# Silu, the convolution's first step and the cast of the gated product issued later, and the first pair's second tile read sooner

## The chip, the cores and the metric

The kernel runs on one core of a Trainium2 chip. The metric is the device time of one execution in microseconds (us). Engines are named as the profile names them: PE does the matmuls (PEld loads their weights), DVE the elementwise work, ACT the activations and plain copies, POOL small copies and sums, SP issues most DMAs. A tile in PSUM is where PE accumulates and where DVE and ACT read results; all other tiles here are in SBUF.

## What is computed

One step of one decoder layer for 512 prompt tokens and 64 sample tokens (8 sequences of 8), 576 columns in all. The change touches only the gated feed-forward part:

```python
h = _rmsnorm(x, norm2_w)
ua, ub = jnp.split(h @ w_up, [D_FF], axis=-1)          # D_MODEL 1024, D_FF 2816
buf = jnp.concatenate([conv_s0.astype(ua.dtype), ua], axis=1)
conv = conv_b
for j in range(CONV_W):                                # CONV_W = 3
    conv = conv + buf[:, j:j + T] * conv_w[j]
x = x + (jax.nn.silu(conv) * ub) @ w_down
```

Before it stand the input projection, retention, attention and the output projection; behind it the final norm.

## The kernel before

**Tiling.** Activations lie transposed: 128 channels on the partitions, 576 token columns. Every f32 matmul is done as three: weight and activation are split into a rounded part and a remainder (`whi`, `wlo`; `hhi`, `hlo` for the normed input; `bhi`, `blo` for the gated product), and PE does hi·hi, hi·lo and lo·hi, each on two halves of 288 columns. A pair of such matmuls is the unit of the traces below. ACT makes `whi` (L289), DVE makes `wlo` (L296); SP loads the raw weights (L250).

**The feed-forward** has 22 channel tiles `f`, in three groups of 8, 8 and 6. For each `f` PE makes two products with the up weights: the first tile (`pa`, the convolution's branch) and the second tile (`pb`, the gate). Tiles 0, 1 and the other odd ones go through `dense` (L341) into PSUM tiles `d`, of which there are two; their elementwise work is `up_post`. Tiles 2, 4, ... 20 (ten of them, called slabs here) go through `up_seven` (L1274), which trades an eighth matmul block for sums, into PSUM tiles `m`; their elementwise work is `post_seven`, and ACT copies parts of `m` out in between (L1280, L1282, L1286). When a group is through, `dense` multiplies its gated products by the down weights, one product (index `n`) after the other.

**The elementwise chain of one f**: `ue` = first tile times the token's norm factor `rstd_b` (L1337, L1338); the convolution's first step on ACT (L1341, in `post_seven` L1301); two more steps on DVE (L1345, L1346; L1310, L1311); Silu on ACT (L1348; L1313); `g` = second tile times `rstd_b` (L1353; L1314); the gated product (L1320, L1321); its cast `bhi` on ACT (L1323) and remainder `blo` on DVE (L1325). The norm factor itself comes from `norm2`: sums over channels, an inverse root, and a broadcast through PE (L415) that DVE copies out (L416, L417).

**What sets the order.** Instructions are not written down in running order. Each chain is a generator, and `Merge` runs them against a planned clock: `yield cost, delay` adds PE cost in ns to that clock and lets this chain go on only after `delay` ns more. Each engine then runs its own instructions strictly in the order in which they were emitted, and waits on semaphores where it must. A delay in a `yield` thus moves an instruction behind others on its engine; it makes nobody wait by itself. PSUM and SBUF slots are given out by the same order: a new `d` tile gets the slot whose last reader was emitted first.

```python
    def add(self, gen, left=None, delay=0.0):
        ...
            self.clock += c[0]
            e["at"] = self.clock + c[1]
```

Of the kernel before, what the change touches and what calls it, by code (L numbers as in the profile page):

```python
# [22 lines left out]
T = NP + NS  # L23
# [123 lines left out]
def decoder_step(ctx, tc, a):  # L147
    nc = tc.nc
    pe, dve, act, pool, sp = nc.tensor, nc.vector, nc.scalar, nc.gpsimd, nc.sync
# [24 lines left out]
    def f32(ap):  # L174
        return ap.bitcast(F32)
# [182 lines left out]
    def tok(ps):  # L358
        return ps[:, C0:C0 + T]
# [27 lines left out]
    rstd_b = cst.tile([P, T], F32, name="rstd_b")  # L387
# [18 lines left out]
    def rstd_cols(dst, ss, n):  # L406
        dve.tensor_scalar(ss, ss, 1.0 / n, EPS, op0=OP.mult, op1=OP.add)
        rsqrt(dst, ss, stat[:, 35:40])

    def row_broadcast(dst, cols):  # L410
        p1, p2 = mtile(), mtile()
        for j in range(5):
            r, s = rows_of(j)
            ps = p1[:, s] if j < 4 else p2[:, :NS]
            pe.transpose(ps, cols[:r, j:j + 1].to_broadcast([r, P]), ident[:r, :r])  # L415
        dve.tensor_copy(dst[:, :NP], p1)  # L416
        dve.tensor_copy(dst[:, NP:], p2[:, :NS])  # L417
# [195 lines left out]
    def keep_rows():  # L613
        if copies:
            act.dma_start(*copies.pop(0))
# [515 lines left out]
    def tmp(name):  # L1131
        return fp.tile([P, UE], F32, name=name, tag="tmp", bufs=6)
# [21 lines left out]
    def token_sums(dst, x):  # L1154
        dve.memset(dst, 1.0)
        ps = mtile()
        for j in range(5):
            r, s = rows_of(j)
            pe.matmul(ps[:r, j:j + 1], x[:, s], ones[:, 0:1], start=True, stop=True)
        dve.tensor_copy(dst[:, 0:4], ps[:, 0:4])  # L1160
        dve.tensor_copy(dst[:NS, 4:5], ps[:NS, 4:5])
# [14 lines left out]
    def norm2():  # L1176
        token_sums(ss2, acc)
        rstd_cols(stat[:, 20:25], ss2, D)
        yield 2200.0, 3700.0
        row_broadcast(rstd_b, stat[:, 20:25])  # L1180
        norm2_made.append(1)
        yield 550.0, 100.0
# [15 lines left out]
    def out_post(m, ps):  # L1198
# [15 lines left out]
        if last:  # L1214
            yield 0.0, 5000.0
            yield from norm2()
# [21 lines left out]
    def seqs(t, off, n):  # L1238
        return t[:, NP + 2:UE].rearrange("p (b t) -> p b t", b=B)[:, :, off:off + n]

    def by_seq(x):
        return x.rearrange("p (b t) -> p b t", b=B)

    def up(f, n, ghi, glo, made):
        if f in SEVEN:
            yield from up_seven(f, n, ghi, glo, made)
            return
        pa = dtile()
        yield from dense(pa, ("up", f), hhis, hlos, 0, KD, True, True, made=h_made)
        pb = dtile()  # L1250
        done = []
        mg.add(up_post(f, n, pa, pb, done, ghi, glo, made), None, 4000.0 if f == 0 else 0.0)
        yield from dense(pb, ("up", NF + f), hhis, hlos, 0, KD, True, True)
        done.append(1)

    def up_seven(f, n, ghi, glo, made):
# [7 lines left out]
        for q, (dst, c) in enumerate(order):  # L1264
            w_begin(j + q)
            if split[j + q][1] is None:
                w_mid(j + q)
            hi, lo = split.pop(j + q)
            xh, xl = TH[c]
            for k in range(4):  # L1270
                while c[0] == "T" and (c, k) not in t_made:
                    yield None
                for wt, b in ((hi, xh), (hi, xl), (lo, xh)):
                    pe.matmul(dst, wt[:, k], b[:, k], start=q in (0, 1, 2, 5) and k == 0 and wt is hi and b is xh,  # L1274
                              stop=k == 3 and wt is lo, skip_group_check=True)
                if k == 0:
                    w_mid(j + q)
                yield 394.0, 0.0
            if q == 0:
                act.copy(ts[0], pa)  # L1280
            elif q == 1:
                act.copy(ts[1], pc)  # L1282
            elif q == 2:
                dve.tensor_tensor(y[:, :H2], pb, ts[0], op=OP.add)
            elif q == 3:
                act.copy(ts[2], pa)  # L1286
            elif q == 4:
                dve.tensor_tensor(y[:, H2:T], pc, ts[2], op=OP.add)
                mg.add(post_seven(f, n, pa, ts[1], y, z, stage, ghi, glo, made))
            elif q == 5:  # L1290
                act.copy(z[:, :H2], pd)
        stage.append(1)

    def post_seven(f, n, pa, t, y, z, stage, ghi, glo, made):
        u, L = ues[f % 2], UE - 2
        pool.tensor_copy(seqs(u, 0, 2), by_seq(csT[:, f]))
        dve.tensor_mul(u[:, 2:NP + 2], y[:, :NP], rstd_b[:, :NP])
        dve.tensor_mul(seqs(u, 2, TS), by_seq(y[:, NP:T]), by_seq(rstd_b[:, NP:]))
        yield 0.0, 1100.0
        c = tmp("cv")  # L1300
        act.activation(c[:, :L], u[:, 0:L], AF.Identity, scale=convw[:, 0, f:f + 1], bias=convb[:, f:f + 1])  # L1301
        pool.tensor_copy(cout[:, 0:2, f], u[:, NP:NP + 2])
        pool.tensor_copy(by_seq(cout[:, 2:, f]), seqs(u, TS, 2))
        while not stage:
            yield None
        yield 0.0, 300.0
        dve.tensor_tensor(z[:, :H2], pa, z[:, :H2], op=OP.add)
        dve.tensor_tensor(z[:, H2:T], pa, t, op=OP.add)
        yield 0.0, 900.0
        dve.scalar_tensor_tensor(c[:, :L], u[:, 1:L + 1], convw[:, 1, f:f + 1], c[:, :L], op0=OP.mult, op1=OP.add)  # L1310
        dve.scalar_tensor_tensor(c[:, :L], u[:, 2:L + 2], convw[:, 2, f:f + 1], c[:, :L], op0=OP.mult, op1=OP.add)  # L1311
        yield 0.0, 1700.0
        act.activation(c[:, :L], c[:, :L], AF.Silu)  # L1313
        dve.tensor_mul(z[:, :T], z[:, :T], rstd_b)  # L1314
        yield 0.0, 900.0
        yield from gated(f, n, z, c, ghi, glo, made)

    def gated(f, n, g, c, ghi, glo, made):

        dve.tensor_tensor(g[:, :NP], g[:, :NP], c[:, :NP], op=OP.mult)  # L1320
        dve.tensor_tensor(by_seq(g[:, NP:T]), by_seq(g[:, NP:T]), seqs(c, 0, TS), op=OP.mult)  # L1321
        yield 0.0, 1000.0
        act.copy(ghi[n], g[:, :T])  # L1323
        yield 0.0, 1500.0
        dve.tensor_sub(glo[n], g[:, :T], f32(ghi[n]))  # L1325
        made[n] = 1
        up_made.append(f)
        if f % 2 == 0:
            keep_rows()

    def up_post(f, n, pa, pb, done, ghi, glo, made):
        u = ues[f % 2]
        ya, L = tok(pa), UE - 2
        while not norm2_made or not cs_made:
            yield None
        pool.tensor_copy(seqs(u, 0, 2), by_seq(csT[:, f]))
        dve.tensor_mul(u[:, 2:NP + 2], ya[:, :NP], rstd_b[:, :NP])  # L1337
        dve.tensor_mul(seqs(u, 2, TS), by_seq(ya[:, NP:]), by_seq(rstd_b[:, NP:]))  # L1338
        yield 0.0, 1800.0
        c = tmp("cv")  # L1340
        act.activation(c[:, :L], u[:, 0:L], AF.Identity, scale=convw[:, 0, f:f + 1], bias=convb[:, f:f + 1])  # L1341
        pool.tensor_copy(cout[:, 0:2, f], u[:, NP:NP + 2])
        pool.tensor_copy(by_seq(cout[:, 2:, f]), seqs(u, TS, 2))
        yield 0.0, 1800.0
        dve.scalar_tensor_tensor(c[:, :L], u[:, 1:L + 1], convw[:, 1, f:f + 1], c[:, :L], op0=OP.mult, op1=OP.add)  # L1345
        dve.scalar_tensor_tensor(c[:, :L], u[:, 2:L + 2], convw[:, 2, f:f + 1], c[:, :L], op0=OP.mult, op1=OP.add)  # L1346
        yield 0.0, 1300.0
        act.activation(c[:, :L], c[:, :L], AF.Silu)  # L1348
        while not done:
            yield None  # L1350
        yield 0.0, 1400.0
        g = tmp("g")
        dve.tensor_mul(g[:, :T], tok(pb), rstd_b)  # L1353
        yield 0.0, 1000.0
        yield from gated(f, n, g, c, ghi, glo, made)

    def conv_state_out():
# [175 lines left out]
```

## Time and profile before

| | us |
|---|---|
| median of 3 runs (824.2 to 825.31) | 824.35 |
| the profiled execution's own time | 825.07 |
| its span in the trace | 823.3 |
| PE busy, 6439 matmuls | 796.0 (97%) |
| DVE busy | 518.2 (63%) |
| ACT busy | 345.0 (42%) |
| down products of the three groups begin at | 493.11, 641.11, 764.84 |

The profiled execution's time is its span and 1.77 us around it. PE is busy nearly all the time, so a change can only gain where PE stands still or runs slowly, and can only lose by making it stand still. Of the views of the trace, the one that lists what PE waited for says where it stood still; the timeline of one engine gives the starts of its instructions, and the distance between two starts, against the same distance in an undisturbed stretch, is what a wait has cost, with the refilling of PE behind it. "Granted clock" in the view by stretches is the share of full speed that PE was given.

### The profile page before, as it was taken

How to read it: one execution, taken by the hardware profiler on the slowest of the kernel's cores; microseconds unless marked ns; L12 is line 12 of the kernel's file. 1: busy time of each engine (PE TensorE's matmuls, PEld its weight loads, DVE VectorE, ACT ScalarE, POOL GpSimd, SP SyncE). 2: the span in 40 equal slices, each digit the busy share in tenths (PEclk: the TensorE clock that was granted, in tenths of full speed). 3: DMA queues.
4: the chain of work that ended last, by engine and by line, in shares of the span. 5: the costliest groups of instructions: out<-in, count | busy, mean ns of one | idle time of the engine just before them, and what ended most of it. 6: DMA issues, size and time to landing. Idle time of an engine off the chain costs nothing.

```text
span 823.3 us, 16179 instructions
## 1 busy us (share of the span) xinstructions
PE 796.0 (97%) x6439; PEld 757.5 (92%) x6439; DVE 518.2 (63%) x1098; ACT 345.0 (42%) x691; POOL 99.0 (12%) x199
## 2 busy tenths in 40 slices
PE   7999999999999999999899999999999999999994
PEld 6999999887888888999799999999999999999994
DVE  5664555665646566787767875347878534778663
ACT  5423232454535567456334452124444312444522
POOL 1311202011110213022001100000110000110021
PEclk9999999999999999999989999999999999999997
DMA  9355653778887863427245554215545621544603
GB/s 268 110 171 140 191 178 96 187 208 220 224 246 207 224 172 103 122 87 251 77 153 180 180 179 152 79 53 179 180 135 174 205 77 52 180 136 147 214 1 115
DMA packets 179673, 128.68 MB, mean 156 GB/s; under 512 B 14849, under 2 KB 176273, under 8 KB 179086
## 3 DMA queue, kind: packets, MB, share of 16 engines
q1 hardware_dynamic: 178445, 93.75, 40.3%
q10 hardware_dynamic: 928, 33.63, 11.3%
q8 instruction: 51, 0.84, 0.4%
q0 software_dynamic: 224, 0.28, 0.1%
q14 instruction: 25, 0.20, 0.1%
HBM read 121.52 MB, written 39.66 MB: 196 GB/s over the span
## 4 chain that ended last, share of the span: by engine, by line
PE 83%; DVE 8%; ACT 3%; issue 3%; DMA 1%; POOL 0%; ACTq 0%; SPq 0%; DVEq 0%; POOLq 0%
PE d L341 52%; PE m L1274 11%; PE m L980 3%; PE d L546 2%; PE m L1025 2%; DVE wlo L296 1%; PE m L907 1%; PE d L990 1%; PE m L894 1%; PE m L593 1%; ACT whi L289 1%; PE px L505 1%; DVE blo L1325 1%; PE px L341 1%; PE m L763 1%
## 5 line engine op out<-in xcount | busy, mean ns | idle before, releaser
L341 PE MATMUL d<-bhi,whi 128*128 128x288 f32 x786 | 176.8, 306 | 2.9 <-ACT bhi L1323 1.7
L341 PE MATMUL d<-blo,whi 128*128 128x288 f32 x786 | 168.1, 295 | 0.8 <-DVE blo L1325 0.8
L341 PE MATMUL d<-bhi,wlo 128*128 128x288 f32 x786 | 168.1, 295 | 0.0
L341 PEld LDWEIGHTS d<-bhi,whi 128*128 128x128 f32 x786 | 124.6, 189 | 8.7 <-issue 3.1
L341 PEld LDWEIGHTS d<-blo,whi 128*128 128x128 f32 x786 | 126.0, 188 | 1.5 <-DVE blo L1325 1.5
L341 PEld LDWEIGHTS d<-bhi,wlo 128*128 128x128 f32 x786 | 126.2, 188 | 0.0
L296 DVE TENSOR_TENSOR wlo<-wraw,whi 128x512 fp32r<-128x512 f32 (+1 forms) x145 | 99.7, 705 | 39.5 <-ACT whi L289 39.3
L289 ACT ACTIVATE whi<-wraw 128x512 fp32r<-128x512 f32 (+1 forms) x145 | 87.3, 619 | 81.2 <-PE d L341 71.8
L341 PE MATMUL d<-hhi,whi 128*128 128x288 f32 x312 | 67.9, 299 | 4.4 <-DVE ue L1338 4.4
L341 PE MATMUL d<-hhi,wlo 128*128 128x288 f32 x312 | 67.7, 298 | 0.0
L341 PE MATMUL d<-hlo,whi 128*128 128x288 f32 x312 | 67.4, 298 | 0.0
L341 PEld LDWEIGHTS d<-hhi,whi 128*128 128x128 f32 x312 | 51.0, 192 | 4.9 <-issue 4.8
L341 PEld LDWEIGHTS d<-hlo,whi 128*128 128x128 f32 x312 | 50.8, 191 | 0.0
L341 PEld LDWEIGHTS d<-hhi,wlo 128*128 128x128 f32 x312 | 50.8, 191 | 0.0
L1274 PE MATMUL m<-T,whi 128*128 128x288 f32 x240 | 48.6, 295 | 0.0
L1389 DVE TENSOR_TENSOR xT<-d,xT 128x576 f32<-128x576 f32 x23 | 17.4, 757 | 40.7 <-PE d L341 40.7
L296 DVE TENSOR_TENSOR wlo<-wrawb,whi 128x512 fp32r<-128x512 f32 (+1 forms) x32 | 22.6, 713 | 28.7 <-ACT whi L289 28.7
L1274 PEld LDWEIGHTS m<-T,whi 128*128 128x128 f32 x240 | 38.4, 188 | 0.2 <-ACT ct L1280 0.2
L1274 PE MATMUL m<-T,wlo 128*128 128x288 f32 x120 | 35.5, 296 | 0.0
L1323 ACT CAST bhi<-g 128x576 fp32r<-128x576 f32 x22 | 14.8, 674 | 49.1 <-DVE g L1321 49.0
L888 POOL TENSOR_SCALAR s<-s,sc 128x128 f32<-128x128 f32 (+3 forms) x32 | 18.3, 579 | 140.4 <-DVE sc L886 125.8
L981 ACT COPY kt<-m 128x384 f32<-128x384 f32 x32 | 15.3, 478 | 39.3 <-PE m L980 37.2
(333 smaller groups left out, 1574.7 us busy)
## 6 DMA issues: line engine op xcount, KB each, us to landing
wraw<-in_w_up_dram SPq DMA_DIRECT2D x33, 512.0 KB, 3.7
wraw<-in_w_in_dram SPq DMA_DIRECT2D x26, 512.0 KB, 6.4
kc<-in_cache_win_k_dram SPq DMA_DIRECT2D x32, 256.0 KB, 3.5
vc<-in_cache_win_v_dram SPq DMA_DIRECT2D x32, 256.0 KB, 3.5
wraw<-in_w_down_dram SPq DMA_DIRECT2D x12, 512.0 KB, 3.5
wrawb<-in_w_up_dram SPq DMA_DIRECT2D x11, 512.0 KB
kc<-in_cache_win_k_dram SPq DMA_DIRECT2D x64, 64.0 KB, 3.3
vc<-in_cache_win_v_dram SPq DMA_DIRECT2D x64, 64.0 KB, 3.1
```

What stands on the lines that cost most here:

```text
L289: act.activation(split[j][0][:, :n], src, AF.Copy)
L296: dve.tensor_sub(split[j][1][:, :n], src, f32(split[j][0][:, :n]))
L341: pe.matmul(ps[:, C0 + s * H2:C0 + (s + 1) * H2], wt[:, x], b[k][:, s * H2:(s + 1) * H2], start=first and k == k0 and wt is hi and b is xh ...
L505: pe.transpose(ps[:, s], xn[:r, j, k * P:(k + 1) * P], ident[:r, :r])
L546: pe.matmul(ps[i][:, C0 + s * H2:C0 + (s + 1) * H2], wt[:, k % 4], x[k][:, s * H2:(s + 1) * H2], start=k == 0 and wt is hi and x is xhis, ...
L888: pool.tensor_scalar(s[:, :n], s[:, :n], c[:, 2:3], 1.0, op0=OP.mult, op1=OP.mult)
L980: pe.transpose(ps[:, j * P:(j + 1) * P], K[u, x][:, 3 * w + j], ident)
L981: (act.copy if w else dve.tensor_copy)(kt[:, w * 384:w * 384 + 384], ps[:, :384])
L1025: pe.matmul(ps[x * 32:(x + 1) * 32, :P], pt[:, j, x * 32:(x + 1) * 32], v, start=j == 0, stop=j == 6, tile_position=(0, x * 32))
L1274: pe.matmul(dst, wt[:, k], b[:, k], start=q in (0, 1, 2, 5) and k == 0 and wt is hi and b is xh, stop=k == 3 and wt is lo, skip_group_chec ...
L1323: act.copy(ghi[n], g[:, :T])
L1389: dve.tensor_add(xT[:, m], tok(ps), xT[:, m])
```

## The change

Five edits, all in the feed-forward:

1. `norm2`: the planned delay before the broadcast of the norm factor is 2300 instead of 3700 ns.
2. `post_seven` (the ten slabs): the convolution's first step is planned 2600 instead of 1100 ns after `ue`, Silu 3400 instead of 1700 ns after the last convolution step, the gated product 1200 instead of 900 ns after that.
3. `gated`: the cast of the product is planned 2200 instead of 1000 ns behind it, except for the last `f` of a group.
4. `up_post`, for `f` = 0 alone: as soon as the second tile is complete, and ahead of the convolution's second and third step, `g` is made from it (new line L1350). For the other `f` it stays where it was (now L1361).
5. `up_post`: Silu is planned 3000 instead of 1300 ns after the last convolution step, except for the last `f` of a group.

```diff
@@ norm2
-        yield 2200.0, 3700.0
+        yield 2200.0, 2300.0
         row_broadcast(rstd_b, stat[:, 20:25])
@@ post_seven
-        yield 0.0, 1100.0
+        yield 0.0, 2600.0
         c = tmp("cv")
...
-        yield 0.0, 1700.0
+        yield 0.0, 3400.0
         act.activation(c[:, :L], c[:, :L], AF.Silu)
         dve.tensor_mul(z[:, :T], z[:, :T], rstd_b)
-        yield 0.0, 900.0
+        yield 0.0, 1200.0
@@ gated
-        yield 0.0, 1000.0
+        yield 0.0, 1000.0 if f == made["last"] else 2200.0
         act.copy(ghi[n], g[:, :T])
@@ up_post
+        g = None
+        if f == 0:
+            while not done:
+                yield None
+            yield 0.0, 500.0
+            g = tmp("g")
+            dve.tensor_mul(g[:, :T], tok(pb), rstd_b)
         yield 0.0, 1800.0
...
-        yield 0.0, 1300.0
+        yield 0.0, 1300.0 if f == made["last"] else 3000.0
         act.activation(c[:, :L], c[:, :L], AF.Silu)
         while not done:
             yield None
         yield 0.0, 1400.0
-        g = tmp("g")
-        dve.tensor_mul(g[:, :T], tok(pb), rstd_b)
-        yield 0.0, 1000.0
+        if g is None:
+            g = tmp("g")
+            dve.tensor_mul(g[:, :T], tok(pb), rstd_b)
+            yield 0.0, 1000.0
```

In the emitted program no instruction is added or taken away. On PE one thing moves: the five transposes of the broadcast (L415), within the last part of the second tile of `f` = 0 (lines with - stand so before, with + after; L341 are matmuls with up weights):

```order
-L341 MATMUL d<-hhi,whi 128x288 x2
-L341 MATMUL d<-hlo,whi 128x288 x2
-L341 MATMUL d<-hhi,wlo 128x288 x2
 L415 MATMUL m<-ident,stat 128x128 x4
 L415 MATMUL m<-ident,stat 128x64
+L341 MATMUL d<-hhi,whi 128x288 x2
+L341 MATMUL d<-hlo,whi 128x288 x2
+L341 MATMUL d<-hhi,wlo 128x288 x2
```

Six such pairs in all, of which three are shown, now stand behind the transposes instead of ahead of them. On SP and POOL nothing changes its place.

DVE at the same place, from the splits of the slabs' input (T, t, h) to the convolution of `f` = 0 (`ue_4467`) and the first product of `f` = 1 (`ue_4469`):

```order
 L1195 TENSOR_TENSOR T<-h,T 128x288
+L1350 TENSOR_TENSOR g<-d,rstd_b 128x576
+L1195 TENSOR_TENSOR T<-h,T 128x288
 L278 TENSOR_TENSOR ws<-ws,wraw 128x512
 L296 TENSOR_TENSOR wlo<-wraw,whi 128x512
-L1195 TENSOR_TENSOR T<-h,T 128x288
-L1345 SCALAR_TENSOR_TENSOR cv<-ue_4467,vec,cv 128x592
-L1346 SCALAR_TENSOR_TENSOR cv<-ue_4467,vec,cv 128x592
+L1352 SCALAR_TENSOR_TENSOR cv<-ue_4467,vec,cv 128x592
+L1353 SCALAR_TENSOR_TENSOR cv<-ue_4467,vec,cv 128x592
```

The read of the second tile (`g<-d`) stood nine rows further down before, behind `ue_4469`. With it the slot of PE's next `d` tile changes, the second tile of `f` = 1. Its first matmuls, with the engines whose semaphores they wait for, before:

```order
L341 MATMUL d_5217<-hhi_4457,whib_5124 128x288 x2
L341 MATMUL d_5217<-hlo_4458,whib_5124 128x288 x2
L341 MATMUL d_5217<-hhi_4457,wlob_5132 128x288 x2
L341 MATMUL d_5297<-hhi_4457,whi_5174 128x288 [waits DVE_49,PE_49,Activation_49]
L341 MATMUL d_5297<-hhi_4457,whi_5174 128x288
```

and after:

```order
L341 MATMUL d_5225<-hhi_4457,whib_5124 128x288 x2
L341 MATMUL d_5225<-hlo_4458,whib_5124 128x288 x2
L341 MATMUL d_5225<-hhi_4457,wlob_5132 128x288 x2
L341 MATMUL d_5298<-hhi_4457,whi_5174 128x288 [waits DVE_49,Activation_49]
L341 MATMUL d_5298<-hhi_4457,whi_5174 128x288
```

`d_5217` and `d_5225` are the first tile of `f` = 1. The new tile waited for PE itself before (for that first tile to be finished), and no longer does.

ACT at the end of the first group (`f` = 6 a slab with `ue_4467`, `f` = 7 the last one with `ue_4469`), before:

```order
L1313 ACTIVATE cv<-cv 128x592
L289 ACTIVATE whi<-wraw 128x512
L1323 CAST bhi<-g 128x576
L1341 ACTIVATE cv<-ue_4469,vec 128x592
L289 ACTIVATE whi<-wraw 128x512
L615 DMA out_dram<-in_cache_win_v_dram 32x16384
L289 ACTIVATE whi<-wraw 128x512
L1348 ACTIVATE cv<-cv 128x592
```

and after:

```order
L289 ACTIVATE whi<-wraw 128x512 x2
L1313 ACTIVATE cv<-cv 128x592
L1341 ACTIVATE cv<-ue_4469,vec 128x592
L289 ACTIVATE whi<-wraw 128x512
L1323 CAST bhi<-g 128x576
L289 ACTIVATE whi<-wraw 128x512
L615 DMA out_dram<-in_cache_win_v_dram 32x16384
L1355 ACTIVATE cv<-cv 128x592
```

The split of a weight piece now stands ahead of the Silu of `f` = 6, and the next split and the first convolution step of `f` = 7 ahead of the cast of `f` = 6. The ends of the other two groups are changed in the same way.

## Rows read from the trace of the kernel before

**Rows 1.** PE's waits from 390 us on: us in total, times, longest.

```profile
PE d L341 <- DVE ue L1338: 4.4, 2, 3.9
PE d L341 <- ACT bhi L1323: 1.7, 3, 0.8
```

**Rows 2.** Stretches: length, busy us of PE, PEld, DVE, ACT, POOL, granted clock, DMA.

```profile
408.40:412.26 3.86, 0.00 (x1) 0.03 (x1) 3.14 (x7) 1.27 (x3) 0.22 (x2) 0.92 0.00 0
412.26:418.20 5.94, 5.94 (x25) 5.94 (x26) 4.79 (x8) 2.25 (x4) 0.25 (x2) 0.50 0.93 323
...
501.00:641.00 140.00, 140.00 (x1056) 139.66 (x1055) 88.27 (x154) 52.68 (x96) 8.05 (x24) 1.00 0.44 138
```

**Rows 3.** The chain that ended last, undisturbed stretches: start us, us, what.

```profile
432.73 12.70 PE d L341 x96
445.43 11.14 PE m L1274 x84
```

**Rows 4.** Timeline of PE, 399 to 422 us: start, us, instruction, [idle before <- releaser].

```profile
399.47 0.80 PE L415 MATMUL m<-ident,stat 128*128 128x128 f32 x5
...
400.83 0.43 PE L341 MATMUL d<-hhi,wlo 128*128 128x288 f32 x2
401.80 0.50 PE L341 MATMUL d<-hhi,whi 128*128 128x288 f32 x2 [0.55 <-DVE ue L1338]
...
412.26 0.82 PE L341 MATMUL d<-hhi,whi 128*128 128x288 f32 x2 [3.86 <-DVE ue L1338]
...
421.47 0.29 PE L1274 MATMUL m<-hhi,whi 128*128 128x288 f32 x1
```

**Rows 5.** Timeline of DVE in the same stretch.

```profile
396.97 0.17 DVE L400 SCALAR_TENSOR_TENSOR stat<-stat 128x5 f32<-128x5 f32 x1
...
400.11 0.69 DVE L416 COPY rstd_b<-m 128x512 f32<-128x512 f32 x1 [2.36 <-PE m L415]
...
401.44 0.21 DVE L1338 TENSOR_TENSOR ue<-d,rstd_b 128x64 f32<-128x64 f32 x1
...
405.76 0.46 DVE L1195 TENSOR_TENSOR T<-h,T 128x288 fp32r<-128x288 f32 x1 [0.57 <-ACT T L1193]
...
407.71 0.83 DVE L1345 SCALAR_TENSOR_TENSOR cv<-ue,vec,cv 128x592 f32<-128x592 f32 x1
...
411.90 0.21 DVE L1338 TENSOR_TENSOR ue<-d,rstd_b 128x64 f32<-128x64 f32 x1
412.03 0.75 DVE L1353 TENSOR_TENSOR g<-d,rstd_b 128x576 f32<-128x576 f32 x1
```

**Rows 6.** Timeline of PE in the first group's down products.

```profile
498.44 0.42 PE L341 MATMUL d<-bhi,wlo 128*128 128x288 f32 x2
499.29 0.53 PE L341 MATMUL d<-bhi,whi 128*128 128x288 f32 x2 [0.43 <-ACT bhi L1323]
...
500.46 0.42 PE L341 MATMUL d<-bhi,wlo 128*128 128x288 f32 x2
```

**Rows 7.** Timeline of PE in the third group's down products.

```profile
770.31 0.53 PE L341 MATMUL d<-bhi,whi 128*128 128x288 f32 x2 [0.80 <-ACT bhi L1323]
```

**Rows 8.** Timeline of ACT and DVE at the end of the first group.

```profile
490.83 0.67 ACT L1323 CAST bhi<-g 128x576 fp32r<-128x576 f32 x1 [2.23 <-DVE g L1321]
...
492.84 0.69 DVE L296 TENSOR_TENSOR wlo<-wraw,whi 128x512 fp32r<-128x512 f32 x1 [2.04 <-ACT whi L289]
...
496.33 0.75 DVE L1353 TENSOR_TENSOR g<-d,rstd_b 128x576 f32<-128x576 f32 x1
```

**Rows 9.** Timeline of ACT at the end of the third group.

```profile
762.58 0.88 ACT L1341 ACTIVATE cv<-ue,vec 128x592 f32<-128x592 f32 x1
...
763.89 1.28 ACT L1484 ACT_TABLE_LOAD   x1
...
765.18 0.20 ACT L1484 ACTIVATE stat<-small 128x1 f32<-128x1 f32 x1
```

**Rows 10.** Timeline of ACT during a slab (`f` = 4).

```profile
449.27 0.39 ACT L1282 COPY ct<-m 128x288 f32<-128x288 f32 x1
```

## The prediction

> **What bounds the kernel now.** I read the page first: PE is busy for 796.0 of 823.3 us, so a change off PE counts only where PE waits for it. The view of PE's waits says where. From 390 us on DVE's `ue` holds PE up twice, 4.4 us together, the longest 3.9, and ACT's `bhi` three times [rows 1]. Between them there is nothing to gain: from 501 to 641 us, with the second group's slabs in it, PE is busy for 140.00 of 140.00 us at granted clock 1.00 [rows 2]. That leaves four places: the passage to the first slab (400 to 422 us) and the three group ends. For the cost of a wait I take starts, not idle time, since a refill follows each. Undisturbed, 96 matmuls take 12.70 us [rows 3], so a pair takes 12.70 / 48 = 0.265 us.
>
> **The passage to the first slab.** From the pair at 400.83 to the first slab matmul at 421.47 there are 20.64 us [rows 4], for the last pair of `f` = 0 and 24 pairs for each tile of `f` = 1: 49 pairs, 12.96 us at full speed. So 7.68 us are lost there, in three ways.
>
> First, 0.55 us idle at 401.80, where the first tile of `f` = 1 needs the slot that `ue` of `f` = 0 reads [rows 4]. `ue` is late because the broadcast is: its transposes run at 399.47 [rows 4], DVE sits 2.36 us for them, copies at 400.11 and starts the last piece of `ue` at 401.44 [rows 5].
>
> Second, 3.86 us idle until 412.26 [rows 4]. DVE's `ue` of `f` = 1 has its last piece at 411.90, and PE goes on at 412.26, although the read of the second tile of `f` = 0 starts at 412.03 and takes 0.75 [rows 5]. So PE did not wait for that read. The tile that it wanted to start lay where the first tile of `f` = 1 itself had just been written, and had to wait until DVE, behind two convolution steps (from 407.71) and weight work, had read that one [rows 5].
>
> Third, the clock. In the idle stretch PE did nothing, and from 412.26 to 418.20 it was granted 0.50, the 1.2 GHz level instead of 2.4 [rows 2]. The second tile of `f` = 1 thus takes 421.47 − 412.26 = 9.21 us for 24 pairs, 6.35 at full speed: 2.86 us. The Trainium skill ("TensorE: Matmul & The Clock Gate", Terms) prices a throttled stretch at its length times one less the share of pulses passed: 5.94 × 0.5 = 2.97. By that the sum below would be 0.1 larger; the starts stand in it.
>
> **Edit 1, the broadcast.** It stands six pairs earlier, 6 × 0.265 = 1.59 us. It needs the last inverse-root step, which starts at 396.97 and takes 0.17 [rows 5]; the new place is 399.47 − 1.59 = 397.88, so PE does not wait, with 0.74 us to spare. The last piece of `ue` then starts at 401.44 − 1.59 = 399.85 and ends by 400.1, and PE wants the slot at 400.83 + 0.265 = 401.1. The first loss goes, and the first tile of `f` = 1 ends near 401.1 + 6.35 = 407.45.
>
> **Edit 4, the early read.** The order shows that the next tile no longer waits for PE's own first tile but for the new read alone. The nine DVE rows between `ue` and that read are those that stood before the split at 405.76, in another order, and the split itself. Before, that split started 4.32 us behind the last piece of `ue` [rows 5]; so it starts at 399.85 + 4.32 = 404.2 and the read ends about 0.4 + 0.75 later, at 405.3; one ACT weight split has come between, at most 0.6 us more. PE wants the slot at 407.45: 1.5 us or more to spare. In DVE's queue the read waits for PE's end of that tile, 401.1, which is long past, so nothing behind it is held. Losses two and three go with it; the price, if the read came x us too late, is x plus its refill, and up to 2.86 if the clock falls again. I take the whole 7.68.
>
> What is late next? Without the 3.86 us and the slow stretch, PE reaches the first slab 7.7 us sooner and DVE must have its weight pieces by then. From 408.40 to 412.26 DVE was busy for 3.14 us and from 412.26 to 418.20 for 4.79 of 5.94 [rows 2]; the two read-and-convolve chains of `f` = 0 and 1 were in it, which the slab does not wait for. I expect no new wait; its bounds are 0 and about 2 us.
>
> **Edits 2, 3 and 5, the later steps.** Within a group they cost nothing: PE's cover is the 140.00 us of rows 2, and a product is first needed in the down matmuls, three pairs per `n`, the seventh (`f` = 6) 6 × 0.79 us after they begin. Without that cover each step's delay would be paid. On SP and POOL nothing is moved past anything; the one DMA that ACT issues there, the cache copy, moves by one row.
>
> At the group ends they clear the path. PE runs out of finished products at `n` = 7: from 498.44 to 500.46 are 2.02 us for three pairs, 0.79 at full speed, so 1.23 us lost [rows 6]; the second group's end has the same waits, 148 us later. In the third the wait for `bhi` is 0.80 instead of 0.43 [rows 6, 7]: 1.23 + 0.37 = 1.60. All would go if `bhi` of the last tile came sooner by 499.29 − (498.44 + 0.265) = 0.59 us in groups one and two, and by 0.80 in the third. Ahead of it DVE sat 2.04 us for an ACT weight split (492.84), and that split stood behind the cast of `f` = 6 (490.83) and the first convolution step of `f` = 7; the last chain on DVE starts at 496.33 [rows 8]. Now convolution step and split stand before the cast. So up to 2.04 us of DVE's idle time go, against 0.59 needed. The second tile of `f` = 7, which this chain reads, is finished at 493.1 and does not bind.
>
> The third group has two table loads on ACT between the cast and the last Silu, the first at 763.89. The convolution step at 762.58 and a split now stand before the cast: 763.89 − 762.58 = 1.31 us less behind it [rows 9], against 0.80 needed: 0.5 us to spare, the tightest of all. Next to that stands the Trainium skill ("ScalarE: Activation LUTs", What ACT_TABLE_LOAD costs): besides the load a drain of about 1.4 us is paid at every switch. The trace disagrees here, the load takes 1.28 us and the next activation starts at 765.18, 0.01 us behind its end [rows 9]. By the page's price, an estimate, the third end would keep its wait and the sum would be 1.6 smaller.
>
> **Sum.** 7.68 + 2 × 1.23 + 1.60 = 11.74 us. The profiled execution took 825.07 (span 823.3 and 1.77 around it), which gives 813.3; it lies 0.72 above the median of the runs, so for the median 824.35 − 11.74 = 812.6.
>
> **Rivals.**
> - *The group ends keep their waits*, because something else sets the last chain, such as Silu and cast, now later, of the tile before. Against it: the split was what DVE waited for. It gives 824.35 − 7.68 = 816.7.
> - *The third end alone keeps its wait*, if ACT's two table loads hold the chain by over 0.5 us more than counted. For it: they are the longest ACT instructions there [rows 9]. Against it: nothing stands idle behind the load. 1.60 us stay: 814.2. The page on ScalarE of the Trainium skill, as cited, would lead here.
> - *The second tile of `f` = 1 still waits*, since the read comes late behind the splits, or the first slab finds its weights late. It decides from 1.5 us of delay on. With 2 us of wait and the clock falling as before, the gain is 11.74 − 2 − 2.86 = 6.9: 817.5; with 3.86 us and the clock, 11.74 − 6.72 = 5.0: 819.3.
> - *The change doesn't do what it says*: the new tile still lies on the wrong slot. Then at most the 0.55 us and its refill, about 0.8, and the group ends are gained: 819.5. The order speaks against it.
> - *Slower.* In each of the ten slabs PE's fifth part needs an ACT copy (L1282) of an earlier one, and a Silu stands ahead of that copy. The copy ran at 449.27 for 0.39; the fifth part begins 4 × 12 matmuls after 445.43, at 445.43 + 48 × 11.14 / 84 = 451.8 [rows 3, 10], so 2.1 us to spare. If the later Silu pushed the copy more than that, ten slabs would pay, and from 2.1 + 1.34 = 3.4 us on they would eat the gain and 1.6 us more: 3.5 us give 10 × 1.4 = 14 us, so 826.6. Silu's own delay is 1.7 us, but in the order the convolution steps that it waits for stand one DVE instruction earlier than before, so it should not be later at all.
>
> **How the numbers follow.** The forecast has a chance of 0.66, the third end kept 0.08, waits at two or more group ends kept 0.10, a wait left in the passage 0.08, no effect of edit 4 0.03, slower 0.03, about no change 0.02. The predicted time is 812.6. The range goes from 811.8 (the runs lie up to 0.15 below their median, and some 0.6 for sizes read too small) to 817.0, which takes in the group ends as they are; about 0.16 is left out. About 0.2% or 1.6 us can be told from no change: faster than that 0.95 (all but the last two cases), within 0.02, slower 0.03.
>
> **What would show it.** Right: no wait of PE on `ue` or `bhi` in the list from 390 us on, a granted clock of 1.00 from 400 to 425 us, the first slab matmul near 413.8, and the new read ending before 406.5. Edit 1 is wrong if PE waits at the broadcast. The group ends are wrong if `bhi` still releases PE. The forecast fails as a whole if PE waits inside slabs, on `ct`, `wlo` or `whi`, where it does not wait now.

## The result, and the profile after

The changed kernel takes 814.46 us (median of 4 runs, 812.67 to 816.0), the kernel before on the same chip 824.83: a ratio of 0.987, interval 0.986 to 0.989, so 10.4 us less. The forecast was 812.6 with a range of 811.8 to 817.0. Direction, case and range held; the time came out 1.9 us above the forecast, and what put it there lies outside the four places of the sum.

On the page of the profiled execution (816.0 us, span 814.2), PE, PEld (its weight loads), DVE, ACT and POOL with busy time, share of the span and instructions:

```profile
PE 794.0 (98%) x6439; PEld 757.0 (93%) x6439; DVE 520.9 (64%) x1098; ACT 348.8 (43%) x691; POOL 110.3 (14%) x199
```

PE is busy for 2.0 us less than before, with the same instructions. What PE waited for from 385 us on (total us, times, longest):

```profile
PE m L1407 <- ACT sq L1446: 1.3, 1, 1.3
```

That is the whole list; the last norm's wait was there before. The waits of [rows 1], for `ue` and for `bhi`, are gone. The stretches that answer to [rows 2], with the busy time of PE, PEld, DVE, ACT and POOL, the granted clock, DMA share and GB/s:

```profile
401.20:408.00 6.80, 6.80 (x52) 6.56 (x51) 5.27 (x13) 2.69 (x6) 0.99 (x3) 1.00 0.01 3
408.00:414.00 6.00, 6.00 (x48) 6.00 (x47) 5.96 (x10) 2.01 (x4) 0.00 (x0) 1.00 0.30 87
414.00:420.00 6.00, 6.00 (x48) 6.00 (x47) 5.30 (x11) 3.67 (x7) 1.47 (x3) 1.00 0.98 339
```

PE does not stand still in the passage and keeps the full clock, 1.00, where it had 0.50 before. The timelines of PE (three rows) and DVE (three), for [rows 4, 5]; an x counts only the matmuls inside the window that was asked for:

```profile
396.75 0.95 PE L1159 MATMUL m<-small,acc 128*128 128x1 f32 x8
401.11 0.80 PE L415 MATMUL m<-ident,stat 128*128 128x128 f32 x5
417.03 0.29 PE L1274 MATMUL m<-hhi,whi 128*128 128x288 f32 x1
...
401.75 0.69 DVE L416 COPY rstd_b<-m 128x512 f32<-128x512 f32 x1 [0.78 <-PE m L415]
403.09 0.22 DVE L1338 TENSOR_TENSOR ue<-d,rstd_b 128x64 f32<-128x64 f32 x1
408.35 0.75 DVE L1350 TENSOR_TENSOR g<-d,rstd_b 128x576 f32<-128x576 f32 x1
```

DVE sits 0.78 us for the transposes instead of 2.36. The early read ends at 409.10; PE wants the slot one undisturbed tile (6.35) ahead of the first slab, at 417.03 − 6.35 = 410.68. So 1.58 us are to spare. The chain that ended last, for [rows 3] and the ends in [rows 6, 7]:

```profile
401.91 15.29 PE d L341 x114
417.19 11.11 PE m L1274 x84
...
475.95 63.77 PE d L341 x480
...
611.19 11.12 PE m L1274 x84
```

A group end is now one piece: 480 matmuls in 63.77 us, the last up tiles and all down products without a break. ACT at the first group's end (three rows, for [rows 8]) and at the third (two, for [rows 9]):

```profile
483.26 0.89 ACT L1341 ACTIVATE cv<-ue,vec 128x592 f32<-128x592 f32 x1 [2.83 <-DVE ue L1338]
484.05 0.61 ACT L289 ACTIVATE whi<-wraw 128x512 fp32r<-128x512 f32 x1
484.80 0.68 ACT L1323 CAST bhi<-g 128x576 fp32r<-128x576 f32 x1
...
756.31 1.28 ACT L1355 ACT_TABLE_LOAD   x1
757.60 0.70 ACT L1355 ACTIVATE cv<-cv 128x592 f32<-128x592 f32 x1
```

Convolution step and weight split stand ahead of the cast, as the order said.

**A ruler for all runs.** I divide every execution by starts of PE's matmuls: from the second norm's sums (L1159) to the first slab is the passage; then come the slabs, the three group ends, and the last norm's first matmul. Before, L1159 starts at 393.52:

```profile
393.52 0.84 PE L1159 MATMUL m<-small,acc 128*128 128x1 f32 x7
```

From there to the last norm there were 410.15 us; in the changed kernel 397.88 (396.75 to 794.63). The gain there is 12.27 us. What lies ahead of L1159 came out 3.23 us longer in this execution. The rest of an execution's own time is 21.3 to 21.5 us in every trace of before, after and the runs below, so start-up, this stretch and 21.4 us add up to each time.

### The profile page after: what moved, and what is told of

It is laid out like the page before. It is cut to its first block, busy times and chain, and to the rows that moved or that the text cites. A ratio compares the mean times of both kernels' runs of the same rounds, so it can differ in the third digit from the quotient of the medians.

```text
span 814.2 us, 16200 instructions
## 1 busy us (share of the span) xinstructions
PE 794.0 (98%) x6439; PEld 757.0 (93%) x6439; DVE 520.9 (64%) x1098; ACT 348.8 (43%) x691; POOL 110.3 (14%) x199
## 4 chain that ended last, share of the span: by engine, by line
PE 95%; ACT 2%; DVE 1%; DMA 1%; issue 0%; POOL 0%; SPq 0%; ACTq 0%; DVEq 0%; POOLq 0%
PE d L341 61%; PE m L1274 14%; PE m L980 3%; PE d L546 2%; PE m L1025 2%; PE m L907 1%; PE d L990 1%; PE m L894 1%; PE m L593 1%; PE px L341 1%; PE m L763 1%; DMA wraw<-in_w_in_dram 1%; PE px L505 1%; PE m L866 1%; PE m L1428 1%; PE d L1013 1%
## 5 line engine op out<-in xcount | busy, mean ns | idle before, releaser
L341 PE MATMUL d<-bhi,whi 128*128 128x288 f32 x786 | 176.5, 306 | 1.2 <-DVE t L654 1.2
L341 PE MATMUL d<-bhi,wlo 128*128 128x288 f32 x786 | 168.3, 296 | 0.0
L341 PE MATMUL d<-blo,whi 128*128 128x288 f32 x786 | 167.6, 295 | 0.0
L341 PEld LDWEIGHTS d<-bhi,whi 128*128 128x128 f32 x786 | 124.7, 189 | 6.3 <-issue 3.1
L341 PEld LDWEIGHTS d<-bhi,wlo 128*128 128x128 f32 x786 | 126.2, 188 | 0.0
L341 PEld LDWEIGHTS d<-blo,whi 128*128 128x128 f32 x786 | 126.1, 188 | 0.0
L341 PE MATMUL d<-hhi,wlo 128*128 128x288 f32 x312 | 66.6, 294 | 0.0
L341 PE MATMUL d<-hhi,whi 128*128 128x288 f32 x312 | 66.5, 294 | 0.0
L341 PE MATMUL d<-hlo,whi 128*128 128x288 f32 x312 | 66.4, 294 | 0.0
L341 PEld LDWEIGHTS d<-hhi,whi 128*128 128x128 f32 x312 | 49.9, 188 | 0.1
L341 PEld LDWEIGHTS d<-hhi,wlo 128*128 128x128 f32 x312 | 49.8, 188 | 0.0
L341 PEld LDWEIGHTS d<-hlo,whi 128*128 128x128 f32 x312 | 49.7, 187 | 0.0
L1302 POOL COPY cout<-ue 128x2 f32<-128x2 f32 x10 | 6.7, 669 | 237.9 <-DVE ue L1297 237.9
L296 DVE TENSOR_TENSOR wlo<-ws,whi 128x512 fp32r<-128x512 f32 x25 | 17.2, 688 | 23.0 <-ACT whi L289 23.0
```

The lines of the kernel that those rows point to most:

```text
L296: dve.tensor_sub(split[j][1][:, :n], src, f32(split[j][0][:, :n]))
L341: pe.matmul(ps[:, C0 + s * H2:C0 + (s + 1) * H2], wt[:, x], b[k][:, s * H2:(s + 1) * H2], start=first and k == k0 and wt is hi and b is xh ...
```

## The experiments

Each run's measured pieces, in us ("slabs" and "ends" are what they take above the changed kernel; ratio against the kernel before on the same chip):

| run | edits | passage | slabs | ends 1, 2, 3 | L1159 to last norm | median | ratio |
|---|---|---|---|---|---|---|---|
| before | none | 27.95 | 0.58 | 1.22, 1.22, 1.58 | 410.15 | 824.83 | |
| after | 1 to 5 | 20.28 | 0 | 0 | 397.88 | 814.46 | 0.987 |
| e1 | 1 to 5 | 20.28 | 0 | 0 | 397.89 | 813.85 | 0.987 |
| e2 | 1, 4 | 20.28 | 3.04 | 1.22, 1.22, 1.33 | 404.69 | 819.87 | 0.994 |
| e3 | 2, 3, 5 | 25.94 | 0 | 0 | 403.54 | 818.97 | 0.992 |
| e4 | 4 | 21.07 | 2.37 | 1.25, 1.24, 1.33 | 404.86 | 820.41 | 0.995 |
| e5 | 1 to 4 | 20.28 | 0 | 0 | 397.88 | 813.46 | 0.987 |
| e6 | 1, 4, 5 | 20.29 | 2.52 | 1.63, 1.60, 2.33 | 405.97 | 821.67 | 0.997 |
| e8 | 5 | 24.39 | 2.53 | 1.44, 1.62, 3.83 | 411.41 | 828.02 | 1.004 |
| e9 | 1, 2, 4 | 20.29 | 0.33 | 0 | 398.23 | 814.27 | 0.987 |
| e10 | 1, 3, 4 | 20.28 | 0 | 0.05, 0, 0 | 397.94 | 814.40 | 0.987 |
| e11 | 1, 2, 3 | 22.11 | 0 | 0 | 399.71 | 815.44 | 0.988 |
| e12 | 1 | 22.10 | 0.64 | 1.25, 1.27, 1.36 | 404.22 | 819.07 | 0.993 |

### The changed kernel again

No edit; only to see whether the 3.23 us ahead of L1159 belong to it.

> The changed kernel once more. The profiled execution of it ran from the token sums of the second norm to its end in 814.2 - 396.9 = 417.3 us, before in 823.3 - 393.7 = 429.6: 12.3 us less, but it reached those sums 3.2 us later, all of it in the first 25 us, where the first weights are loaded and the two programs are alike. Theory A: that start moves from execution to execution in either kernel, so the gain is 11.7 to 12.3 us when starts are alike and the median over many rounds lies 10 to 12 us below before (ratio 0.985 to 0.988). Rival B: the changed program starts late every time: the sums stand at 395 us or later in this trace too, and the gain is 9 to 10.5.

Measured: L1159 at 394.11, the time 813.85 (813.33 to 815.88). Over all profiled executions L1159 starts between 392.82 (e2) and 396.75 (after). Theory A holds for the spread; the stretch behind L1159 repeats within 0.01 us. PE's rows of the first 21 us show where the start-ups part. The same two pairs of the input projection, at 11.98 and 15.89 in before (first two rows), stand at 12.88 and 19.18 in after (the others, with two rows from between):

```profile
11.98 0.56 PE L546 MATMUL d<-blo,whi 128*128 128x288 f32 x2
15.89 0.54 PE L546 MATMUL d<-bhi,whi 128*128 128x288 f32 x2
...
12.88 0.68 PE L546 MATMUL d<-blo,whi 128*128 128x288 f32 x2
17.21 0.68 PE L546 MATMUL d<-blo,whi 128*128 128x288 f32 x2
17.69 0.68 PE L546 MATMUL d<-bhi,wlo 128*128 128x288 f32 x2
19.18 0.53 PE L546 MATMUL d<-bhi,whi 128*128 128x288 f32 x2
```

The first comes 0.90 us later in after, where PE has waited 0.4 us for ACT and ACT's longest wait for weights is 4.3 us against 3.1. To the second there are 3.91 us in before and 6.30 in after, for the same matmuls and without idle time of PE. In after pairs start 0.48 us apart (17.21, 17.69) until some 18 us, in before 0.26 from 12.38 on. A distance of 0.48 is also that of e8's pairs at 774.17 and 774.65, where 0.50 is granted (row further down). So PE stayed at the lower of its two levels (1.2 and 2.4 GHz) for longer, which is 2.39 of the 3.23 us. I read this from the starts; the column of the granted clock gives 1.00 there. From the matmul at 20.75 in before's trace to L1159 each of the 13 traces takes 372.7 to 372.8 us, so all of the spread arises in the first 21 us.

Median less 21.4 less the stretch, if the stretch repeats as it does in after and e1, gives a start-up of 393.3 for before, 393.5 for e12, 393.8 for e2 (both further down) and 394.0 to 395.2 for the others, after among them. So the changed kernels start up 0.2 to 1.9 us later in their medians, though the instructions are the same there. The traces show that PE reaches full speed at another time in each execution; why it should be later in the median stays open.

### The passage alone, the ends alone, the early read alone

e2 is edits 1 and 4, e4 edit 4, e3 the others:

```diff
e2 (e4 without the first pair)
-        yield 2200.0, 3700.0
+        yield 2200.0, 2300.0
+        g = None
+        if f == 0: ... dve.tensor_mul(g[:, :T], tok(pb), rstd_b)
e3
-        yield 0.0, 1100.0      # and 1700, 900 in post_seven
+        yield 0.0, 2600.0      # and 3400, 1200
-        yield 0.0, 1000.0      # gated
+        yield 0.0, 1000.0 if f == made["last"] else 2200.0
-        yield 0.0, 1300.0      # up_post
+        yield 0.0, 1300.0 if f == made["last"] else 3000.0
```

> Edits 1 and 4 alone. Theory A (the four places are separate): PE's two waits on ue and the 0.50 clock go, 7.7 us less than before, ratio about 0.9907; PE still waits for bhi at all three group ends (1.7 us in the list). Rival: the group ends were late only because everything behind the passage was late; then those waits are gone too and the time is that of the whole change, ratio 0.986.

> Edit 4 alone, the early read of f = 0's second tile; the broadcast stays late. Theory A (the slot): the 3.9 us wait and the slow clock go, the 0.55 us wait stays, group ends stay: 7.7 - 0.8 = 6.9 us less, ratio about 0.9916. Rival (DVE is simply too late there and the earlier broadcast is what helps): the second tile of f = 1 still waits 1.5 us or more, and the gain is under 5.5 us, ratio over 0.9933.

> Edits 2, 3 and 5 alone. Theory A: no wait for bhi at the group ends, 4.1 us less than before, ratio about 0.995; the waits on ue (3.9 us) and the stretch at clock 0.50 stay. Rival: moving the slab's steps later changes nothing at the ends by itself: ratio 1.000 and three waits for bhi.

All three missed. e2 and e4 gained less than expected, e3 more. e4's time is the one that its rival gives, but the wait of the second tile that the rival needs is not in its list. The passage in e2 is the full change's, 20.28, but a wait stands in PE's list that neither kernel has (e2, from 385 us on):

```profile
PE d L341 <- ACT bhi L1323: 1.4, 3, 0.6
PE m L1274 <- ACT ct L1280: 1.3, 3, 0.6
```

Two rows of ACT's timeline of e2, in the slab that starts at 437.25, then one of PE there, then ACT in the same slab (`f` = 4) of before (start 445.27) and of the full change (start 440.84):

```profile
441.72 0.70 ACT L1355 ACTIVATE cv<-cv 128x592 f32<-128x592 f32 x1 [2.52 <-DVE cv L1353]
442.32 0.38 ACT L1280 COPY ct<-m 128x288 f32<-128x288 f32 x1
442.75 0.53 PE L1274 MATMUL m<-T,whi 128*128 128x288 f32 x2 [0.56 <-ACT ct L1280]
...
448.45 0.38 ACT L1280 COPY ct<-m 128x288 f32<-128x288 f32 x1
...
442.64 0.40 ACT L1280 COPY ct<-m 128x288 f32<-128x288 f32 x1 [4.28 <-PE m L1274]
443.46 0.69 ACT L1355 ACTIVATE cv<-cv 128x592 f32<-128x592 f32 x1
```

In e2 the copy that PE's fourth part needs stands behind the Silu of the odd tile, which waits for DVE. PE was there at 442.19, when its matmul before ended, 4.94 us into the slab; the copy ended at 442.70, 5.45 into it. Before, the copy stood behind the same Silu, but ended 3.56 us into the slab (448.45 + 0.38 − 445.27), 1.38 us early. The instructions are no slower. Counted from L1159, PE reaches this slab 7.3 us sooner than before (44.43 against 51.75), but the copy starts only 5.4 us sooner (49.50 against 54.93): the elementwise chains of the first tiles do not come forward by as much as PE. Each of the two slabs loses about 1.03 us. In e4 the passage is 0.79 us longer, which is what I had counted for edit 1, and the slabs wait nearly as much.

e3 shortens the passage by 2.0 us without edits 1 and 4. PE's hold (first row, its busy time is 0.01) and the clock after it:

```profile
408.98:412.08 3.10, 0.01 (x1) 0.03 (x1) 3.06 (x7) 0.74 (x2) 0.21 (x2) 1.00 0.00 0
412.08:414.00 1.92, 1.92 (x10) 1.92 (x11) 1.65 (x3) 1.35 (x2) 0.25 (x2) 0.68 0.04 9
414.00:416.00 2.00, 2.00 (x10) 2.00 (x10) 1.97 (x5) 0.00 (x0) 0.00 (x0) 0.50 0.22 65
416.00:418.00 2.00, 2.00 (x16) 2.00 (x16) 0.99 (x2) 1.14 (x2) 0.00 (x0) 0.95 0.67 198
```

The hold lasts 3.10 instead of 3.86 us, and the slow stretch is shorter: the second tile of `f` = 1 takes 7.96 us (412.08 to the slab at 420.04) instead of 9.21. So 0.76 and 1.25 us.

### Which of the later steps is needed

e5 is the full change without edit 5, e6 the full change without 2 and 3, e8 edit 5 alone:

```diff
e5: changed kernel, up_post
-        yield 0.0, 1300.0 if f == made["last"] else 3000.0
+        yield 0.0, 1300.0
e6: changed kernel, post_seven and gated as before
e8: kernel before, up_post
-        yield 0.0, 1300.0
+        yield 0.0, 1300.0 if f == made["last"] else 3000.0
```

> Edits 1, 2, 3 and 4; edit 5 (the later Silu of the odd tiles) is undone. Theory A: it is edit 5 that keeps the slabs free in the full change, since it puts Silu (L1355) behind ACT's copy L1280 that PE's fourth part needs. Then PE waits for ct from L1280 again, about 1.0 us in each of the slabs f = 4 and 6 and 0.3 to 0.7 in some others, while the passage keeps its 7.7 us and the group ends stay free: 397.9 + about 2.5 = 400.4 us from the second norm's sums to the tail, 816.5 us. Theory B: edit 2 or 3 is the cover (the later convolution step lets the odd tile's chain pass). Then no wait for ct, 397.9 us, 813.9 us. Theory C: edit 5 is what clears the group ends: then bhi waits come back there as well, 3 x 1.3 us more than A, 820 us.

> Edits 1, 4 and 5; the slabs' delays and the cast's delay are undone. Theory A (edit 5 covers the slabs, edits 2 and 3 clear the group ends): no wait for ct, slabs at 23.8 us a pair of tiles; PE waits for bhi at the three ends, 1.2, 1.2 and 1.6 us with the refill: 402 us from the second norm's sums to the tail, 817.5 us. Theory B (edits 2 and 3 cover the slabs): the ct waits stay too, 404.7 us, 820 us. Theory C (edit 5 clears the ends as well, since Silu then stands behind the weight split that the last chain wants): 398 us, 813.9 us.

> Edit 5 alone. Theory A: the hold in the passage shortens by itself, as it did with edits 2, 3 and 5 (idle 3.1 us instead of 3.86, the second tile of f = 1 in 8.0 us instead of 9.2), because an ACT weight split comes ahead of Silu and DVE gets it sooner: passage 25.9 us instead of 27.95; the group ends keep their waits for bhi; 408 us from the sums to the tail, 823 us. Theory B: the shorter hold came from edit 3 (the cast of f = 0 and 1 out of the way), so with edit 5 alone the passage stays at 27.95: 825.0 us. Theory C: the ends go too: 404 us, 819 us.

My theory, that edit 5 covers the slabs by putting Silu behind the copy, fell at once: without edit 5 the stretch takes 397.88 us, the same as with it. With 5 and without 2 and 3 the wait only goes elsewhere (e6):

```profile
PE d L341 <- ACT bhi L1323: 3.2, 3, 1.5
...
PE m L1274 <- ACT ct L1286: 0.6, 2, 0.3
```

The wait is now for a later copy, L1286, and the ends get longer than in e2: 1.6, 1.6 and 2.3 us; none of e6's theories has that. Edit 5 alone shortens the passage by 3.6 us, all of theory A and more, and loses more than that at slabs and ends: from L1159 on it takes 1.26 us longer than before. Its median, 828.02 us, is slower than before, ratio 1.004 (1.003 to 1.006), which none of its theories had; the rest of the difference lies in start-up. e8's PE row at the hold, the stretch behind it, and the same two at its third end:

```profile
413.01 0.50 PE L341 MATMUL d<-hhi,whi 128*128 128x288 f32 x2 [3.10 <-DVE ue L1338]
...
413.20:415.20 2.00, 2.00 (x17) 2.00 (x17) 1.73 (x4) 1.17 (x2) 0.06 (x1) 1.00 0.04 8
...
771.58 0.53 PE L341 MATMUL d<-bhi,whi 128*128 128x288 f32 x2 [1.54 <-ACT bhi L1323]
...
774.00:776.00 2.00, 2.00 (x10) 2.00 (x10) 0.80 (x2) 1.10 (x2) 0.00 (x0) 0.50 0.59 174
```

The hold is 3.10 us, exactly e3's. So edit 5 is what shortened it there, too; but here the clock stayed at 1.00 afterwards and the second tile took 6.42 us (413.01 to 419.43). So of the 3.56 us that the passage gains 0.76 are the shorter hold and 2.79 the clock, in the one execution that was traced. At the third end it was the other way round: PE stood 1.54 and 0.26 us, as in e6 (1.53 and 0.26), but in e8 the clock then fell to 0.50, and the end cost 3.83 us instead of e6's 2.33.

### Edit 2 or edit 3

```diff
e9: kernel before with edits 1, 4, and in post_seven
-        yield 0.0, 1100.0      # and 1700, 900
+        yield 0.0, 2600.0      # and 3400, 1200
e10: kernel before with edits 1, 4, and in gated
-        yield 0.0, 1000.0
+        yield 0.0, 1000.0 if f == made["last"] else 2200.0
```

> Edits 1, 2 and 4; edits 3 and 5 are undone. In the runs with 1 and 4 the wait in the slabs and the wait at the group ends have one cause: the cast of the even tile's product (ACT, L1323) waits for DVE's product, the weight split and the convolution step of the odd tile stand behind that cast, and DVE waits for the split with the odd tile's convolution behind it. Theory A: edit 2 alone puts convolution step and split ahead of the cast, so it clears both the slabs and the ends: 397.9 us from the second norm's sums to the tail, no wait of PE but the one for sq, 813.7 us. Theory B: edit 3, which delays the cast itself, is needed for one of them: the slabs f = 4 and 6 at 24.8 (2 us more) or the ends at 52.3 and 38.6 (3.8 us more), 816 to 820 us.

> Edits 1, 3 and 4; edits 2 and 5 are undone. By the emitted order edit 3 alone puts the cast behind the odd tile's convolution step, but still ahead of the weight split. Theory A: the split then comes about 0.8 us sooner (one convolution step), so DVE's chain does too: the slabs f = 4 and 6 lose about 0.2 instead of 1.0 us each, the first two ends are free (0.59 us were needed), the third is at its edge: 398.4 to 399.5 us from the sums to the tail, 814.5 to 815.5 us. Theory B: the split must pass the cast as well, nothing is gained: 404.7 us as with 1 and 4 alone, 820 us. Theory C: edit 3 alone is enough for all: 397.9 us, 813.7 us.

Either is enough. With edit 2 alone 0.33 us stay in one slab, with edit 3 alone 0.05 at one end. No kernel beats the full change from L1159 on; e5 equals it with one edit fewer. e10 came out better than its theory A, at the number of its theory C. ACT in the slab that starts at 437.25 in e2 (first three rows) and at 439.01 in e10 (last three):

```profile
436.69 0.68 ACT L1323 CAST bhi<-g 128x576 fp32r<-128x576 f32 x1 [3.32 <-DVE g L1321]
437.27 0.88 ACT L1341 ACTIVATE cv<-ue,vec 128x592 f32<-128x592 f32 x1
438.06 0.61 ACT L289 ACTIVATE whi<-wraw 128x512 fp32r<-128x512 f32 x1
...
437.15 0.89 ACT L1341 ACTIVATE cv<-ue,vec 128x592 f32<-128x592 f32 x1 [2.65 <-DVE ue L1338]
437.94 0.66 ACT L1323 CAST bhi<-g 128x576 fp32r<-128x576 f32 x1
438.50 0.63 ACT L289 ACTIVATE whi<-wraw 128x512 fp32r<-128x512 f32 x1
```

In e2 ACT sits 3.32 us for the product that the cast wants, with convolution step and split behind it. In e10 the convolution step runs in that time, and the split starts 0.51 us ahead of the slab instead of 0.81 behind its start: 1.32 us sooner, where I had counted one convolution step. DVE, for the split, in the slab (first two rows: e2, e10) and at the first group's end (e6 with the cast ahead, e10 with it behind the convolution step):

```profile
438.70 0.69 DVE L296 TENSOR_TENSOR wlo<-wraw,whi 128x512 fp32r<-128x512 f32 x1 [1.44 <-ACT whi L289]
439.16 0.69 DVE L296 TENSOR_TENSOR wlo<-wraw,whi 128x512 fp32r<-128x512 f32 x1 [0.77 <-ACT whi L289]
...
486.58 0.69 DVE L296 TENSOR_TENSOR wlo<-wraw,whi 128x512 fp32r<-128x512 f32 x1 [2.05 <-ACT whi L289]
485.24 0.69 DVE L296 TENSOR_TENSOR wlo<-wraw,whi 128x512 fp32r<-128x512 f32 x1 [1.38 <-ACT whi L289]
```

At the end DVE waits 0.67 us less (2.05 − 1.38), against the 0.59 that the prediction had as needed: enough, by a hair, and 0.05 us are left in the table. So slab waits and end waits have one cause, ACT's cast ahead of the work that the next tile's chain needs; in the slabs it costs time only where PE also comes early, as e12 below shows.

### The broadcast with and without the early read

```diff
e11: changed kernel, edits 4 and 5 undone (the read stays in its old place)
e7, e12: kernel before, norm2
-        yield 2200.0, 3700.0
+        yield 2200.0, 2300.0
```

> Edits 1, 2 and 3; the early read (edit 4) and edit 5 are undone. By the emitted order the read of f = 0's second tile stands ahead of the product of f = 1 even so, since edit 1 alone shifts the plan, but behind two convolution steps and a weight split. Theory A: the right slot is what counts, and the read comes 2 to 3 us later than with edit 4: PE waits 1 to 1.5 us for it, the clock stays: passage 21.3 to 22 us instead of 20.28, 815 us. Theory B: edit 4 adds nothing to edit 1: passage 20.3, 397.9 us, 813.7 us. Theory C: the hold is long enough for the clock to fall: passage 23.5 to 25 us, 817 to 818.5 us.

> Edit 1 alone. Theory A: the idle 0.55 us at the first tile of f = 1 goes, with its refill 0.79 us, and the long hold behind it stays as long as it was, since DVE's product of the first tile of f = 1 cannot start before PE has made that tile: passage 27.95 - 0.79 = 27.16 us from the sums to the slab f = 2, the clock at 0.50 as before; 824.2 us. Theory B: DVE is the late one in that hold (its queue, not PE, sets when that product ends), so what PE gains in front it loses in the hold: passage 27.95 us, 825.0 us. Theory C: DVE's queue comes forward by the 1.6 us of the broadcast and the hold shrinks: 25.5 to 26.5 us, 823.0 us.

> Edit 1 alone once more, for its trace: its profiled execution before ran throughout with matmuls over three times as long as in any other run and says nothing of waits. Theory A: edit 1 alone takes most of the passage (20.3 to 22 us instead of 27.95, the tile of f = 1 no longer on the slot of its own first tile), and the slabs f = 4 and 6 then lose about 1 us each to ct, the ends keep their waits: 405 to 406 us from the sums to the tail. Theory B: the passage gains only 4 to 5 us and the slabs lose nothing.

e7 gave four times, 819.53 to 820.6 us, but no trace to read: its profiled execution, with matmuls over three times as long as anywhere else, took 2696.14 us and is left out. e12 is the same kernel and gave the trace. Edit 1 alone is worth 5.85 us in the passage, not the 0.8 that I had counted: with the plan 1.4 us ahead, the read of `f` = 0's second tile is emitted ahead of the product of `f` = 1 even without edit 4, so the new tile lies on the right slot. Edit 4 brings the read forward. In e11 (PE, then DVE, then PE's idle stretch and the one after it):

```profile
410.28 0.50 PE L341 MATMUL d<-hhi,whi 128*128 128x288 f32 x2 [1.58 <-DVE g L1353]
409.38 0.75 DVE L1353 TENSOR_TENSOR g<-d,rstd_b 128x576 f32<-128x576 f32 x1
...
408.70:410.28 1.58, 0.00 (x1) 0.03 (x1) 1.58 (x4) 0.81 (x2) 0.00 (x0) 1.00 0.00 0
410.28:412.28 2.00, 2.00 (x15) 2.00 (x16) 2.00 (x5) 0.12 (x1) 0.28 (x1) 1.00 0.04 8
```

The read ends 15.53 us behind L1159 (410.13 − 394.60), in the full change 12.35 behind it. It is 3.18 us later; 1.58 were to spare; the difference, 1.60, is the wait of 1.58. With its refill it costs 1.83 us, and the clock stays at 1.00. That is theory A's mechanism, just past its range.

In e12, with the order of e2 in its slabs but a passage 1.82 us longer, the slabs `f` = 2 and 4 lose nothing; the copy ends 3.58 us into the slab, as before. Neither of e12's theories holds whole: the passage is as in A, just past its range, the slabs are as in B. e12 is thus 0.47 us shorter than e2 from L1159 to the last norm: without edits 2 or 3 the early read loses in the slabs more than the 1.82 us that it gains.

## Why the prediction was right, and where not

- **Passage:** 7.68 predicted, 7.67 measured (27.95 − 20.28). The three losses were read rightly, and so was the spare time of the read: "1.5 us or more", traced 1.58, and e11 confirms it by taking it away. The first slab came 20.28 us behind L1159, as 413.8 would be in a trace that starts up like before's (393.52 + 20.28 = 413.80).
- **Which edit does it:** here a step of the working failed. I gave edit 1 the first loss (0.55 us and its refill) and edit 4 the other two. Alone, edit 1 gains 5.85 us and edit 4 gains 6.88; either puts the tile on the right slot. Had I emitted the order of edit 1 alone, I should have seen it.
- **Group ends:** 1.23, 1.23 and 1.60 predicted, 1.22, 1.22 and 1.58 measured, by the way described. The third, which I called the tightest, is free with edit 2 or 3 alone.
- **"I expect no new wait":** true of the whole change, but for a reason that the working didn't have. Without edits 2 and 3 the faster passage brings 2.46 us of new waits in the slabs (3.04 − 0.58 in e2), beyond the bound of about 2 that I gave. "Within a group they cost nothing" was half the account: there edits 2 and 3 earn these 2.46 us. I had also picked the wrong copy for the rival that ends slower. L1282 had 2.1 us to spare, L1280, one earlier, 1.38; and what eats that time is not a later Silu but an earlier PE.
- **The sum misses 0.58 us.** In the last slab ahead of the first two group ends PE lost 0.17 and 0.42 us before (in the starts of slabs, 24.01 and 24.26 against 23.84). The second lies in the stretch of [rows 2] that shows PE busy for 140.00 of 140.00 us: ends of matmuls are modelled, so short waits vanish in busy time. The chain had it:

```profile
617.01 11.55 PE m L1274 x84
```

  11.55 us for the 84 matmuls that take 11.12 after. With it the measured parts add up: 7.67 + 1.22 + 1.22 + 1.58 + 0.58 = 12.27.
- **The level:** 12.27 us are gained from L1159 on, the medians differ by 10.4. By the ruler the missing 1.9 lie ahead of L1159, in start-up, which the working took as equal. That is the term that put the forecast 1.9 us too low; the 0.53 us that the sum missed and the 0.48 by which before's median came out higher (824.83 against 824.35) cancel.
- **The clock:** the rival "2 us of wait and the clock falling as before" put 2.86 us for the clock beside the wait. In e11, with 1.58 us of wait, they were not paid; at e8's third end, with 1.54 and 0.26 us, the clock fell. So whether 2 us would have cost them is not shown. The Trainium skill ("TensorE: Matmul & The Clock Gate", Terms) prices a slow stretch by its length and the pulses withheld; for e3 that is 1.92 × 0.32 + 2.00 × 0.50 + 2.00 × 0.05 = 1.71, an estimate, and by the starts 7.96 − 6.35 = 1.61: it agrees within 0.1, as in the kernel before.
- **The table loads:** the next activation starts 0.01 us behind the load's end again (756.31 + 1.28, 757.60), and the load 0.02 us behind the activation before it. The drain that the Trainium skill ("ScalarE: Activation LUTs", What ACT_TABLE_LOAD costs) adds at a switch is not seen, and the third end is free.

## What to carry to other kernels

When one stage gets shorter, the engines that feed the next stage need not get earlier by as much: list for that next stage, for each operand PE takes, how early it was, and subtract the gain. Look at the queue for an instruction that waits with others' work behind it, here ACT's cast; moving it down by one or two places cleared two kinds of waits at once. Emit each edit of a change alone, since in a planned order one delay can do another's work, and measure short waits by starts, not by busy time.

## What the runs showed of the hardware that I had not expected

- After the same hold of 3.10 us at PE the granted clock fell to 0.68 and 0.50 in e3 and stayed at 1.00 in e8. At the third end, after 1.54 and 0.26 us in e8 it fell to 0.50, after 1.53 and 0.26 us in e6 it stayed. After 1.58 us in e11 it stayed, with the 3.86 us of before it fell. Idle time alone does not tell whether it falls; what else decides was not settled.
- The start-up differs by up to 3.9 us between executions (L1159 at 392.82 to 396.75), more than most of the waits here, while the 398 us behind it repeat within 0.01 us in the kernel that ran twice. Most of the difference between before and after is how long PE stays at half speed at first (pairs 0.48 us apart until about 12 us in one, 18 us in the other). So of two kernels compare a stretch by its starts first.
